# Input transfers, first norm and weight splits at the head of a hybrid decoder step on one Trainium2 core

## The chip, the cores and the metric

The kernel runs on 1 core of one Trainium2 chip. A core has five engines that run their own instruction streams: TensorE (PE in the profile, with its weight loads as PEld), VectorE (DVE), ScalarE (ACT), GpSimd (POOL) and SyncE (SP, which here only issues transfers). 16 DMA engines move data between the chip's memory and the core's SBUF; matmul results lie in PSUM, here eight banks of 128 partitions x 512 float32. The metric is the device time of one execution in microseconds (us), as a median of several runs.

## The reference, cut to what matters

The program is one layer of a decoder trunk with a final norm, for 1024 prompt rows and 64 sample rows (8 sequences of 8) of width 1024. The head of the kernel, with which this change deals, is the first norm and the first gated feed-forward block:

```python
def rmsnorm(x, w):
    xf = x.astype(jnp.float32)
    y = xf * lax.rsqrt(jnp.mean(xf * xf, axis=-1, keepdims=True) + EPS)
    return (y * w.astype(jnp.float32)).astype(x.dtype)

def ffn_half(x, nw, wg, wu, wd):
    h = rmsnorm(x, nw)
    return x + 0.5 * ((jax.nn.silu(h @ wg) * (h @ wu)) @ wd)

def layer(x, q_pos, past, prm, is_prompt):
    x = ffn_half(x, prm['norm_ffn1'], prm['ffn1_wg'], prm['ffn1_wu'], prm['ffn1_wd'])
    h = rmsnorm(x, prm['norm_mix'])
    ...
    x = x + jnp.concatenate([o_att, y_ssm], axis=-1) @ prm['w_out']
    x = ffn_half(x, prm['norm_ffn2'], prm['ffn2_wg'], prm['ffn2_wu'], prm['ffn2_wd'])
```

`wg` and `wu` are 1024 x 2816, `wd` is 2816 x 1024, all float32. Between the two feed-forward blocks stand sparse attention and a state-space mixer, which the change does not touch.

## The kernel before

**Rows.** The 1088 rows (1024 prompt, 64 sample) are kept as columns of transposed tiles. They form two halves of 544 (`HALF`), and each half is cut into a first part of 256 and a second of 288 (`SUBS`, line 27). The four chunks start at rows 0, 544, 256 and 800 and are loaded in that order (`XCHUNKS`, line 29).

**Precision.** A float32 product is made of three passes over rounded numbers. Each operand is split (`split`, line 281) into a high part, a cast on ScalarE (line 267), and a low part, the rest after the cast, by a subtraction on VectorE (line 270). The names are `whi` and `wlo` for weights and `B1h`, `B1l` and so on for the activations. The three passes are the matmuls of lines 412 to 414 in the head, and lines 366 to 368 or 633 to 635 later.

**Products.** Gate, up and down are computed by a scheme with seven products of half-size blocks in place of eight. Each pair of row halves gives seven factors B1 to B7 of which four (1, 2, 4, 3) are blocks of h themselves and the rest are sums and differences. The first pair of weight blocks (`class First`, line 388) works with the four plain blocks alone, so that it can begin while the other factors are still made.

**The head, in order of the code.** `x_load` (line 140) issues the transfers of the x chunks on SP: the first two chunks of 1 MB each, one transfer each (line 146). Then `raw0`, the first 256 columns of `wg` as 1 MB (line 160), then the other two chunks. The first x chunk lies in a buffer that later takes the first weights of `wu` (tag `raw`, two buffers), which are issued when that chunk is done with (line 520).

`begin1` (line 740) makes the norm of the first part of each half: `x_rms` for rows 0 and for rows 544. `x_rms` (line 668) squares each row in two halves of 512 with ScalarE's accumulation (line 677), adds the halves (line 680) and calls `norm_rows` (line 222): scale and add (line 224, VectorE), root (line 225, ScalarE), reciprocal (line 226, VectorE), and matmuls with the identity that spread the inverse over all partitions as `xR` (line 228), from where ScalarE copies it (line 683).

`x_block` (line 685), for kk = 0 to 3, transposes the columns kk and kk + 4 of both halves by matmul (line 693), multiplies by the inverse and the norm's weight to the four blocks h (line 695, VectorE), copies the plain transpose to a stage buffer (`stg`, line 696, ScalarE) and issues its store to `xD` on ScalarE's queue (line 698). `b_quad` (line 292) then splits the four h to B1, B2, B4 and B3. After each block, `g.run` (line 395) splits a quarter of the raw weights and does 24 matmuls; `b_rest` (line 296) makes the other factors. Then `wu` follows for the first part (`u.run`), then the norm and blocks of the second parts, and the remaining weight pairs in `gate_up` (line 463).

**The order on the engines.** Each engine runs its instructions in a fixed order. That order is worked out when the program is built: a planner simulates the program with its own costs and, whenever an engine is free in its simulation, gives it the instruction that stands earliest in the code among those that are ready. So an instruction that is ready early can be placed ahead of one that stands earlier in the code. `tc.issue_after(ins)` adds an edge: instructions made inside it, on the engine of `ins`, are placed behind `ins`. `roots` (line 220) collects the root instructions of the norms for such edges (line 752).

Transposes and squares write to four PSUM banks of tag Y (`banky`), the first gate sums to four of tag X (`bankx`).

Of the kernel before, what the change touches and what calls it, by code (L numbers as in the profile page):

```python
# [3 lines left out]

# [10 lines left out]
AF = mybir.ActivationFunctionType  # L15
OP = mybir.AluOpType
AX = mybir.AxisListType

P = 128
# [6 lines left out]
HALF = T // 2  # L26
# [54 lines left out]
def hybrid_step(ctx: ExitStack, tc: tile.TileContext, *aps):  # L81
    nc = tc.nc
# [57 lines left out]
    def x_load(t0, n):  # L140
        first = not xrows
        xt = (F1R if first else F1).tile([P, 2, DM], F32, name="xt", tag="raw" if first else "Cc",
                                         bufs=2 if first else 3)
        m = min(n, TP - t0, 2 * P) - P
        if m == P:
            nc.sync.dma_start(xt, A["x_prompt"][0, t0:t0 + 2 * P].rearrange("(u p) d -> p u d", p=P))
        else:
            nc.sync.dma_start(xt[:, 0], A["x_prompt"][0, t0:t0 + P])
            nc.sync.dma_start(xt[:m, 1], A["x_prompt"][0, t0 + P:t0 + P + m])
        xrows[t0] = [(xt[:, 0], 0, 0, P), (xt[:, 1], 0, P, m)]  # L150
        if t0 + n == HALF:
            nc.sync.dma_start(xrest[:32], A["x_prompt"][0, t0 + 2 * P:HALF])
            xrows[t0].append((xrest, 0, 2 * P, 32))
        elif t0 + n == T:
            nc.sync.dma_start(xrest[64:], xs2)
            xrows[t0].append((xrest, 64, P + m, 64))
    for t0, n in XCHUNKS[:2]:
        x_load(t0, n)
    raw0 = f32(F1R.tile([P, 8, 2 * P], F32R, name="raw", tag="raw", bufs=2))
    nc.sync.dma_start(raw0, A["ffn1_wg"][0][:, :2 * P].rearrange("(k p) f -> p k f", p=P))  # L160
    for t0, n in XCHUNKS[2:]:
        x_load(t0, n)
    ident = C.tile([P, P], F32, name="ident")
# [23 lines left out]
    def banky(name):  # L187
        return PS.tile([P, 512], F32, name=name, tag="Y", bufs=4)
# [28 lines left out]
    def blocks(n):  # L217
        return [(i, min(P, n - P * i)) for i in range((n + P - 1) // P)]

    roots = []  # L220

    def norm_rows(r, parts, R):

        nc.vector.tensor_scalar(r, r, 1.0 / DM, EPS, op0=OP.mult, op1=OP.add)
        root = nc.scalar.activation(r, r, AF.Sqrt)
        nc.vector.reciprocal(r, r)
        for i, p0, c0, m in parts:
            nc.tensor.matmul(R[:, c0:c0 + m], r[p0:p0 + m, i:i + 1].to_broadcast([m, P]), ident[p0:p0 + m, p0:p0 + m],
                             start=True, stop=True, skip_group_check=True)
        roots.append(root.ins)  # L230
        return R

    def wsplit(W, loads, early=False, dve=False):
# [58 lines left out]
    def b_quad(z, kk, h):  # L292
        for i, src in zip((1, 2, 4, 3), h):
            b_put(z, kk, i, src)
# [373 lines left out]
    def x_rms(t0, n):  # L668
        r = K.tile([P, 3], F32, name=f"xr{t0}", bufs=1)
        r2 = K.tile([P, 2, 3], F32, name=f"xq{t0}", bufs=1)  # L670
        nc.vector.memset(r2, 1.0)
        R = banky("xR")
        parts = []
        for i, (xt, p0, c0, m) in enumerate(xrows[t0]):
            for z in range(2):
                sq = banky("xsq")
                nc.scalar.activation(sq[p0:p0 + m], xt[p0:p0 + m, 512 * z:512 * z + 512], AF.Square,
                                     accum_out=r2[p0:p0 + m, z, i:i + 1])
            parts.append((i, p0, c0, m))
        nc.vector.tensor_tensor(r, r2[:, 0], r2[:, 1], op=OP.add)  # L680
        norm_rows(r, parts, R)
        Rs[t0] = FX.tile("xRs", [P, 288], 2)
        nc.scalar.copy(Rs[t0][:, :n], R[:, :n])

    def x_block(s, kk):
        c0, n = SUBS[s]
        h = []
        for t0 in (c0, HALF + c0):
            stage[t0] = FX.tile("stg", [P, 2, 288], 2)
            for k in (kk, kk + 4):  # L690
                q = banky("x_ps")
                for xt, p0, o, m in xrows[t0]:
                    nc.tensor.transpose(q[:, o:o + m], xt[p0:p0 + m, P * k:P * k + P], ident[p0:p0 + m, p0:p0 + m])
                v = T4[s][:, kk] if len(h) == 1 else FX.tile(f"h{len(h)}", [P, 288], 2)[:, :n]
                nc.vector.scalar_tensor_tensor(v, q[:, :n], w0[:, k:k + 1], Rs[t0][:, :n], op0=OP.mult, op1=OP.mult)
                nc.scalar.copy(stage[t0][:, k // 4, :n], q[:, :n])
                h.append(v)
            stored.append(nc.scalar.dma_start(xD[:, kk::4, t0:t0 + n], stage[t0][:, :, :n]).ins)
        b_quad(s, kk, h)
        h[1] = None  # L700
        return kk, h

    stage, stored = {}, []

    def x_sub(s, product):
        c0, n = SUBS[s]
        T4[s] = F1H.tile([P, 4, n], F32, name=f"T4{s}")
        due = []
        for kk in range(4):
            due.append(x_block(s, kk))  # L710
            product(kk)
            if kk in (1, 2):
                b_rest(s, *due.pop(0))
        return due
# [24 lines left out]

    def begin1():  # L740
        g = First(F1, w1g, silu_out, raw0)
        for t0 in (0, HALF):
            x_rms(t0, SUBS[0][1])
        due = x_sub(0, lambda kk: g.run(0, kk, bankx, True))
        u = First(F1, w1u, times_out(g))
        c0, n = SUBS[1]
        for kk in range(3):
# [1785 lines left out]
```

## Time and profile before

| | us |
|---|---|
| median of 3 runs | 2473.87 |
| lowest and highest of them | 2472.63, 2479.4 |
| the profiled execution | 2475.45 |
| its span, first to last instruction | 2473.8 |

The profile is of one execution. In its rows, a group of like instructions is given with its line, engine, operation, the tile that it writes and those that it reads, and a count; `[x <-ACT y L677]` means that the engine had been idle for x us and that an instruction of line 677 on ScalarE ended the wait. SPq and ACTq are the queues on which SP and ScalarE issue transfers. A stage of the span can be read on its own, with the busy time of every engine and the granted clock of TensorE (1.00 is full speed; the mean of this execution is 0.987). The rows themselves stand in the prediction.

### The profile page before, as it was taken

The page shows a single profiled execution, that of the slowest core. Times are in us where ns is not written, and L with a number is a line of the kernel's source. Part 1 is how long each engine was busy: PE and PEld are TensorE (multiplying, and loading weights), DVE is VectorE, ACT ScalarE, POOL GpSimd, SP SyncE. Part 2 cuts the span into 40 slices and gives each one's busy share as a digit, 9 for nine tenths or more (in the row PEclk, how much of TensorE's full clock was granted, in tenths as well). Part 3 has the DMA queues.
Part 4 walks back from the last instruction along what each step waited for, and adds up shares of the span by engine and source line. Part 5 has one row for each costly group of instructions (what it writes and reads, how often), then busy time and mean ns, then how long its engine had stood idle before and what let it go on. Part 6 is the DMA issues. An engine that isn't in the chain of part 4 may idle for free.

```text
span 2473.8 us, 48193 instructions
## 1 busy us (share of the span) xinstructions
PE 2408.8 (97%) x19026; PEld 2222.8 (90%) x19026; DVE 1744.7 (71%) x3673; ACT 1131.2 (46%) x2501; POOL 418.3 (17%) x533
## 2 busy tenths in 40 slices
PE   7999999999999999999999999999999999999998
PEld 6999999999999998997667766677899999999998
DVE  6777776677778855655656666777967676768776
ACT  7544444441133254425666675444545454543113
POOL 0000000011134343333434343111000000001110
PEclk9999999999999999999999998999999999999999
DMA  4334343598652333423110104476235353559654
GB/s 162 134 133 160 130 164 129 175 338 306 230 190 84 126 116 102 119 69 127 40 64 35 69 35 148 130 250 213 89 123 171 120 174 120 174 213 370 238 209 153
DMA packets 230446, 379.07 MB, mean 153 GB/s; under 512 B 18509, under 2 KB 147705, under 8 KB 228812
## 3 DMA queue, kind: packets, MB, share of 16 engines
q1 hardware_dynamic: 210248, 318.02, 37.7%
q0 software_dynamic: 7600, 38.59, 4.5%
q10 hardware_dynamic: 12372, 19.38, 2.2%
q8 instruction: 150, 2.46, 0.4%
q14 instruction: 76, 0.62, 0.1%
HBM read 255.66 MB, written 124.40 MB: 154 GB/s over the span
## 4 chain that ended last, share of the span: by engine, by line
PE 86%; DVE 6%; DMA 4%; ACT 3%; issue 1%; POOL 0%; ACTq 0%; DVEq 0%; POOLq 0%
PE dq L634 6%; PE gY L367 6%; PE dq L633 6%; PE dq L635 6%; PE gY L368 6%; PE gY L366 6%; PE gX L367 5%; PE gX L366 5%; PE gX L368 5%; PE o L1855 3%; PE pT L1846 3%; PE s L1808 1%; PE xbc L250 1%; PE xbc L251 1%; PE xbc L252 1%; PE cA L1733 1%
## 5 line engine op out<-in xcount | busy, mean ns | idle before, releaser
L634 PE MATMUL dq<-db,da 128*128 128x256 f32 (+1 forms) x1232 | 353.2, 288 | 0.3 <-DVE da L270 0.3
L635 PE MATMUL dq<-db,da 128*128 128x256 f32 (+1 forms) x1232 | 352.8, 288 | 0.0
L633 PE MATMUL dq<-db,da 128*128 128x256 f32 (+1 forms) x1232 | 349.8, 288 | 2.7 <-DVE Cc L386 2.2
L642 DVE TENSOR_TENSOR xT<-xT,dq 128x256 f32<-128x256 f32 (+1 forms) x456 | 186.9, 432 | 84.8 <-PE dq L635 83.2
L270 POOL TENSOR_TENSOR ds<-dw 128x512 f32<-128x512 f32 x22 | 29.5, 1341 | 1228.1 <-DVE wlo L270 508.0
L633 PEld LDWEIGHTS dq<-db,da 128*128 128x128 f32 x1232 | 230.5, 189 | 3.3 <-DVE Cc L386 2.5
L635 PEld LDWEIGHTS dq<-db,da 128*128 128x128 f32 x1232 | 232.8, 189 | 0.0
L634 PEld LDWEIGHTS dq<-db,da 128*128 128x128 f32 x1232 | 231.9, 188 | 0.6 <-DVE da L270 0.5
L267 ACT CAST whi<-ws 128x512 fp32r<-128x512 f32 x156 | 96.5, 623 | 205.9 <-PE gY L368 137.6
L270 DVE TENSOR_TENSOR wlo<-raw,whi 128x512 fp32r<-128x512 f32 x184 | 125.5, 687 | 83.9 <-ACT whi L267 83.5
L267 ACT CAST da<-ds 128x512 fp32r<-128x512 f32 x88 | 52.6, 623 | 234.7 <-PE dq L635 93.4
L267 ACT CAST whi<-raw 128x512 fp32r<-128x512 f32 x181 | 112.4, 626 | 72.0 <-PE g L414 19.5
L270 DVE TENSOR_TENSOR wlo<-ws,whi 128x512 fp32r<-128x512 f32 x156 | 106.7, 687 | 42.4 <-ACT whi L267 41.9
L1824 ACT ACTIVATE pb<-s,mx 128x256 f32<-128x256 f32 (+3 forms) x192 | 105.0, 552 | 59.7 <-DVE mx L1822 37.6
L1846 PEld LDWEIGHTS pT<-ident,pb 128*128 128x128 f32 x528 | 59.6, 143 | 45.8 <-issue 40.1
L1821 DVE TENSOR_REDUCE mx<-s 128x1 f32<-128x384 f32 (+2 forms) x128 | 66.6, 536 | 44.0 <-PE s L1813 34.1
L366 PE MATMUL gY<-B3h,whi 128*128 128x256 f32 (+1 forms) x320 | 91.5, 287 | 1.5 <-ACT whi L267 1.4
L366 PE MATMUL gX<-B6h,whi 128*128 128x256 f32 (+1 forms) x320 | 91.3, 286 | 0.9 <-ACT Cc L373 0.9
L367 PE MATMUL gX<-B6h,wlo 128*128 128x256 f32 (+1 forms) x320 | 91.4, 286 | 0.6 <-DVE wlo L270 0.6
L367 PE MATMUL gY<-B3h,wlo 128*128 128x256 f32 (+1 forms) x320 | 91.6, 287 | 0.2 <-DVE wlo L270 0.2
L277 POOL TENSOR_TENSOR pb<-pb,sm 128x640 f32<-128x640 f32 (+7 forms) x70 | 85.1, 1238 | 37.6 <-DVE sm L1831 34.0
L367 PE MATMUL gY<-B2h,wlo 128*128 128x256 f32 (+1 forms) x320 | 91.4, 286 | 0.0
(763 smaller groups left out, 8548.1 us busy)
## 6 DMA issues: line engine op xcount, KB each, us to landing
db<-GD SPq DMA_DIRECT2D x42, 1632.0 KB
GD<-Cc SPq DMA_DIRECT2D x154, 272.0 KB
GD<-his SPq DMA_DIRECT2D x84, 272.0 KB
raw<-in_ffn_wu_dram SPq DMA_DIRECT2D x22, 1024.0 KB
dw<-in_ffn_wd_dram SPq DMA_DIRECT2D x44, 512.0 KB
raw<-in_ffn_wg_dram SPq DMA_DIRECT2D x21, 1024.0 KB
GD<-hp SPq DMA_DIRECT2D x70, 272.0 KB
db<-GD SPq DMA_DIRECT2D x14, 1088.0 KB
```

The costliest lines, as they stand in the source:

```text
L267: return nc.scalar.copy(out, src) if eng == "a" else ENGINES[eng].tensor_copy(out, src)
L270: ENGINES[eng].tensor_tensor(out, x, y, op=op)
L277: nc.gpsimd.tensor_tensor(out, x, by.to_broadcast(list(x.shape)), op=OP.mult)
L366: nc.tensor.matmul(q, ah[:, k], b_, start=first, stop=False, skip_group_check=True)
L367: nc.tensor.matmul(q, al[:, k], b_, start=False, stop=False, skip_group_check=True)
L368: nc.tensor.matmul(q, ah[:, k], c_, start=False, stop=(k == 3), skip_group_check=True)
L633: nc.tensor.matmul(q, x, bh[:, u, o], start=first, stop=False, skip_group_check=True)
L634: nc.tensor.matmul(q, y, bh[:, u, o], start=False, stop=False, skip_group_check=True)
L635: nc.tensor.matmul(q, x, bl[:, u, o], start=False, stop=(u == np_ - 1), skip_group_check=True)
L642: nc.vector.tensor_tensor(x, x, q, op=OP.subtract if i == 4 else OP.add)
L1824: nc.scalar.activation(pb[:, st:st + pn], s, AF.Exp, bias=mx[:, 0:1], accum_out=part[:, hh_, i:i + 1])
L1846: nc.tensor.transpose(tq_[:kn, P * hh_:P * hh_ + P], src, ident)
```

## The change

Five edits, all in the head.

1. The chunks of x that start a half (rows 0 and 544) come in two transfers of 128 rows each. The first weights come in four transfers: transfer k brings the row blocks k and k + 4, which `g.run` for kk = k reads.
2. In `x_rms`, the second half of each row is squared on VectorE (`tensor_tensor_reduce`) where the chunk starts a half; ScalarE squares the first half.
3. The norm of a chunk is made inside `x_block`, when its rows are first needed: the block of rows 0 stands ahead of the norm of rows 544.
4. The splits of h (`b_quad`) and the split of the first weights stand behind the second norm's root on ScalarE and behind its reciprocal on VectorE.
5. The weight splits for kk = 1 to 3 stand behind the last stage copy (ScalarE) and the last h (VectorE) of the block before.

```diff
@@ x_load
-        if m == P:
+        if t0 % HALF and m == P:
             nc.sync.dma_start(xt, A["x_prompt"][0, t0:t0 + 2 * P].rearrange("(u p) d -> p u d", p=P))
         else:
             nc.sync.dma_start(xt[:, 0], A["x_prompt"][0, t0:t0 + P])
@@
-    nc.sync.dma_start(raw0, A["ffn1_wg"][0][:, :2 * P].rearrange("(k p) f -> p k f", p=P))
+    for k in range(4):
+        nc.sync.dma_start(raw0[:, k::4], A["ffn1_wg"][0][:, :2 * P].rearrange("(k p) f -> p k f", p=P)[:, k::4])
@@
-    roots = []
+    roots, inverses = [], []
+
+    @contextmanager
+    def behind(pair):
+        with tc.issue_after(pair[0]), tc.issue_after(pair[1]):
+            yield
@@ norm_rows
-        nc.vector.reciprocal(r, r)
+        inverse = nc.vector.reciprocal(r, r)
...
         roots.append(root.ins)
+        inverses.append(inverse.ins)
@@ x_rms
-                sq = banky("xsq")
-                nc.scalar.activation(sq[p0:p0 + m], xt[p0:p0 + m, 512 * z:512 * z + 512], AF.Square,
-                                     accum_out=r2[p0:p0 + m, z, i:i + 1])
+                sq, x = banky("xsq")[p0:p0 + m], xt[p0:p0 + m, 512 * z:512 * z + 512]
+                if z and t0 % HALF == 0:
+                    nc.vector.tensor_tensor_reduce(out=sq, in0=x, in1=x, scale=1.0, scalar=0.0, op0=OP.mult,
+                                                   op1=OP.add, accum_out=r2[p0:p0 + m, z, i:i + 1])
+                else:
+                    nc.scalar.activation(sq, x, AF.Square, accum_out=r2[p0:p0 + m, z, i:i + 1])
@@ x_block
         for t0 in (c0, HALF + c0):
+            if t0 not in Rs:
+                x_rms(t0, n)
...
-                nc.vector.scalar_tensor_tensor(v, q[:, :n], w0[:, k:k + 1], Rs[t0][:, :n], op0=OP.mult, op1=OP.mult)
-                nc.scalar.copy(stage[t0][:, k // 4, :n], q[:, :n])
+                made = nc.vector.scalar_tensor_tensor(v, q[:, :n], w0[:, k:k + 1], Rs[t0][:, :n],
+                                                      op0=OP.mult, op1=OP.mult)
+                staged = nc.scalar.copy(stage[t0][:, k // 4, :n], q[:, :n])
                 h.append(v)
+            ends[s, kk] = staged.ins, made.ins
...
-        b_quad(s, kk, h)
+        with behind((roots[1], inverses[1])):
+            b_quad(s, kk, h)
...
-    stage, stored = {}, []
+    stage, stored, ends = {}, [], {}
@@ begin1
-        for t0 in (0, HALF):
-            x_rms(t0, SUBS[0][1])
-        due = x_sub(0, lambda kk: g.run(0, kk, bankx, True))
+        def gate(kk):
+            with behind(ends[0, kk - 1] if kk else (roots[1], inverses[1])):
+                g.run(0, kk, bankx, True)
+        due = x_sub(0, gate)
```

More of the change, by code (lines that the diff above doesn't have):

```diff
@@ L1 @@
 import itertools
-from contextlib import nullcontext
+from contextlib import contextmanager, nullcontext
 from contextlib import ExitStack
```

## The prediction

> **What bounds the kernel now.** First the page: busy time by engine, and the chain of work that ended last by engine.
>
> ```profile
> PE 2408.8 (97%) x19026; PEld 2222.8 (90%) x19026; DVE 1744.7 (71%) x3673; ACT 1131.2 (46%) x2501; POOL 418.3 (17%) x533
> ...
> PE 86%; DVE 6%; DMA 4%; ACT 3%; issue 1%; POOL 0%; ACTq 0%; DVEq 0%; POOLq 0%
> ```
>
> TensorE is busy for 2408.8 of 2473.8 us, so 65.0 us in all can be won by filling its gaps. Next, the busy time by stage (columns: stage, length, then busy us and instructions of PE, PEld, DVE, ACT, POOL, granted clock, DMA share, GB/s).
>
> ```profile
> 0.00:16.00 16.00, 2.45 (x9) 2.10 (x10) 4.30 (x19) 9.13 (x25) 0.96 (x8) 1.00 0.90 320
> 16.00:36.00 20.00, 16.88 (x123) 15.02 (x122) 19.24 (x53) 14.82 (x46) 0.00 (x0) 1.00 0.54 169
> 36.00:62.00 26.00, 24.73 (x181) 21.31 (x179) 19.34 (x53) 22.07 (x62) 0.00 (x0) 1.00 0.19 58
> 62.00:73.00 11.00, 9.77 (x39) 8.55 (x40) 11.00 (x30) 5.92 (x17) 0.00 (x0) 0.53 0.24 83
> 73.00:90.00 17.00, 17.00 (x130) 17.00 (x130) 9.53 (x19) 8.58 (x19) 0.00 (x0) 1.00 0.46 142
> 90.00:2474.00 2384.00, 2337.98 (x18553) 2158.81 (x18551) 1681.34 (x3502) 1070.69 (x2336) 417.37 (x525) 0.99 0.45 153
> ```
>
> The change touches the head alone. There TensorE does 2.45 us of work in the first 16 us: the norm's inverse is late. From 16 to 36 VectorE is full (19.24 of 20) and TensorE waits for its low parts; from 36 on TensorE is nearly full. So the head is worth what it can start earlier, and every later stage follows as it is, if nothing in it is tied to absolute time. The timeline says why the head starts late (start, length, engine, line, output<-inputs, count, idle time before and what ended it).
>
> ```profile
> 0.83 0.95 SPq L146 DMA_DIRECT2D xt<-in_x_prompt_dram  x2
> ...
> 1.82 0.47 SPq L160 DMA_DIRECT2D raw<-in_ffn_wg_dram  x1
> ...
> 5.92 0.60 ACT L677 ACTIVATE xsq<-xt 128x512 f32<-128x512 f32 x1 [2.93 <-DMA xt<-in_x_prompt_dram]
> ...
> 8.51 0.16 DVE L680 TENSOR_TENSOR xr<-xq 128x3 f32<-128x3 f32 x1 [5.68 <-ACT xsq L677]
> ...
> 9.02 0.58 ACT L677 ACTIVATE xsq<-xt 128x512 f32<-128x512 f32 x1
> 9.15 0.18 DVE L226 RECIPROCAL xr<-xr 128x3 f32<-128x3 f32 x1 [0.27 <-ACT xr L225]
> ...
> 11.47 0.35 ACT L683 COPY xRs<-xR 128x256 f32<-128x256 f32 x1
> ...
> 11.72 2.18 ACT L267 CAST whi<-raw 128x512 fp32r<-128x512 f32 x4
> 11.79 0.17 DVE L224 TENSOR_SCALAR xr<-xr 128x3 f32<-128x3 f32 x1
> 12.37 2.50 DVE L270 TENSOR_TENSOR wlo<-raw,whi 128x512 fp32r<-128x512 f32 x4 [0.41 <-ACT whi L267]
> 13.80 0.20 ACT L225 ACTIVATE xr<-xr 128x3 f32<-128x3 f32 x1
> 14.79 0.17 DVE L226 RECIPROCAL xr<-xr 128x3 f32<-128x3 f32 x1
> 15.01 1.22 PE L228 MATMUL xR<-ident,xr 128*128 128x128 f32 x4 [4.41 <-DVE xr L226]
> ...
> 16.70 0.48 DVE L695 SCALAR_TENSOR_TENSOR h<-x_ps,w,xRs 128x256 f32<-128x256 f32 x1 [1.74 <-PE x_ps L693]
> ...
> 17.62 0.88 DVE L695 SCALAR_TENSOR_TENSOR h<-x_ps,w,xRs 128x256 f32<-128x256 f32 x2
> ...
> 18.41 0.42 DVE L270 TENSOR_TENSOR B1l<-h,B1h 128x256 fp32r<-128x256 f32 x1
> ```
>
> ScalarE waits for the first whole megabyte of x until 5.92, then squares eight half rows alone, four for each norm. The second norm's sum is scaled at 11.79, yet its root comes only at 13.80: four weight casts (11.72 to 13.80) stand ahead of it on ScalarE. Its reciprocal comes at 14.79, as four low parts (12.37 to 14.87) stand ahead of it on VectorE. The first h follows at 16.70.
>
> **The change part by part.**
>
> *Smaller transfers.* When would the pieces land? The DMA view of the first 18 us, in 40 slices of 0.45 us:
>
> ```profile
> GB/s 0 0 0 0 118 27 255 400 428 428 419 392 391 400 419 419 437 355 378 380 355 344 355 391 364 437 410 391 400 401 319 264 364 382 401 218 246 300 246 9
> DMA packets 2255, 5.51 MB, mean 306 GB/s; under 512 B 135, under 2 KB 1167, under 8 KB 2255
> ```
>
> Adding slices, 1.05 MB have moved at 5.25; the square starts at 5.92, so about 0.6 us pass between last byte and use (estimate). If the transfers run in the order of their issue, 0.52 MB are through at 4.0, 1.57 at 6.55, 2.10 at 7.8; the four half transfers are then usable at 4.6, 5.9, 7.15 and 8.4, the four weight quarters at 9.1, 9.8, 10.6 and 11.3 (2.36, 2.62, 2.88 and 3.15 MB at 8.5, 9.2, 10.0 and 10.7). SP issues eight instead of three at 0.47 us each, done by about 4.6, ahead of the data; bytes are the same. The other chunks stand behind them on SP as before; the last slices show them in by 18, and their first square comes at 31.73 (row further down). I cost the issues at nothing. If the pieces land only together, the norms' blocks are there at 5.9 and 8.4, and the second norm ends about 0.6 us later, since its two squares on each engine then follow each other.
>
> [...]
>
> From these rows the fixed part of the first transfer is 1.9 us ahead of its data (issued at 0.83, data from the slice at 2.7 on) and 0.6 behind it. Yet from 3.15 to 13.5 the slices run on at 344 to 437 GB/s across the borders of the transfers, so I take it as overlapped.
>
> *Half the squares on VectorE.* A square on ScalarE goes by 0.61 us (5.92 to 8.51 for four). The tensor_tensor_reduce is not in the trace; its nearest rows are a two-input instruction of the same width, and a custom one, and a wider one with three inputs:
>
> ```profile
> L270 DVE TENSOR_TENSOR wlo<-raw,whi 128x512 fp32r<-128x512 f32 x5 | 3.2, 686 | 0.4 <-ACT whi L267 0.4
> ...
> L2080 DVE CUSTOM_DVE_ANT_0 S<-s_ps,big 128x512 f32<-128x512 f32 x20 | 13.7, 685 | 3.1 <-PE s_ps L2077 3.0
> ...
> L1056 DVE SCALAR_TENSOR_TENSOR acc<-xr,vec,acc 128x1024 f32<-128x1024 f32 x24 | 35.5, 1480 | 0.2
> ```
>
> I take 0.69, with ends of 0.69 and 1.48; VectorE is idle there (4.30 of 16 us busy), so the four cost nothing unless they are slow. First norm: second block at 5.9, squares done at 6.6, then what runs from 8.51 to 9.33 before (add, scale, root, reciprocal: 0.82, with 0.03 to start): 7.45. Second: block at 8.4, squares 9.1, inverse 9.95; call it 10.0, with a little for the first norm's copy. Before: 14.96. At 1.48 each, four from 4.6 on that wait for their data end at 10.1, and the inverse at 11.0.
>
> *Casts and low parts behind the second inverse, block 0 of x ahead of the second norm.* The four casts leave the path to the root (2.1 us), the four low parts that to the reciprocal (0.99 us from the root's start to the reciprocal's). After the inverse the order xR, copy, h stays: 1.74 us (14.96 to 16.70), so the second pair of h starts at 11.75. The first pair (2 x 0.43 us, as four took from 16.70 to 18.41) is now done before it, and B1l, B2l (2 x 0.36, the mean of 53 in 19.24 us) and the first low part (0.62, a quarter of 2.50) fit into the 1.74. Of VectorE's stretch that ran from 16.70 to 36.0, 1.6 us are thus done ahead; but three low parts (3 x 0.62 = 1.9 us) that lay in idle time before now lie inside it. It ends at 11.75 + 19.3 - 1.6 + 1.9 = 31.35, 4.65 us earlier. If nothing is done ahead, 32.95: 3.05 us. If everything hides, 10.0 against 14.96: 4.96 us. I take 4.5, a little under the sum, as the stretch is 96% and not wholly full. Moved casts: three of 0.52 us on ScalarE, which has 5.2 us free from 16 to 36.
>
> What is late next? The up projection's first weights:
>
> ```profile
> 18.19 0.63 ACTq L698 DMA_DIRECT2D xD<-stg  x1
> ...
> 20.81 0.65 ACT L696 COPY stg<-x_ps 128x256 f32<-128x256 f32 x2 [0.46 <-DMA xD<-stg]
> ...
> 27.18 0.38 SPq L520 DMA_DIRECT2D raw<-in_ffn_wu_dram  x1
> ...
> 31.16 0.38 ACT L696 COPY stg<-x_ps 128x256 f32<-128x256 f32 x1 [1.78 <-DMA xD<-stg]
> ...
> 31.73 0.61 ACT L677 ACTIVATE xsq<-xt 128x512 f32<-128x512 f32 x1
> ...
> 33.81 0.43 DVE L267 CAST whi<-raw 128x512 fp32r<-128x512 f32 x1
> ```
>
> They take the buffer of the first x chunk, so they are issued when its last transposes are done (27.18) and are used at 33.81. Both are tied to the blocks, not to the clock, and move with them. The waits added order only ScalarE and VectorE: behind the held casts stand the casts of B and the stage copies, which need the inverse themselves.
>
> *Sum.* 2475.45 (the profiled execution, span 2473.8 and 1.65 around it) - 4.5 = 2470.95. The shown median, 2473.87, lies 1.58 below that execution; so the predicted median is **2469.4**, a change of 0.18%. Less than 0.3%, 7.4 us, can't be told from no change here.
>
> **The rivals.**
>
> *The clock drop goes.* Shorter windows (columns as above):
>
> ```profile
> 28.00:30.00 2.00, 1.11 (x10) 0.94 (x8) 2.00 (x7) 1.05 (x3) 0.00 (x0) 1.00 0.98 271
> ...
> 61.00:62.00 1.00, 0.22 (x2) 0.11 (x1) 1.00 (x4) 0.64 (x2) 0.00 (x0) 1.00 0.00 0
> 62.00:63.00 1.00, 0.00 (x0) 0.00 (x0) 1.00 (x3) 0.27 (x2) 0.00 (x0) 0.72 0.00 0
> 63.00:64.00 1.00, 0.77 (x3) 0.44 (x3) 1.00 (x4) 0.57 (x3) 0.00 (x0) 0.50 0.00 0
> ...
> 72.00:73.00 1.00, 1.00 (x7) 1.00 (x7) 1.00 (x4) 0.00 (x0) 0.00 (x0) 0.66 0.00 0
> ```
>
> After a gap of 2 us TensorE runs at 0.50 for 10 us, and falls behind by up to 4.7 us of work. VectorE is full until 73, so not all of it counts: 130 matmuls stood after 73, 96 of them the up product that comes last anyway; at full clock some 23 of the other 34 would have been done, 23 x 0.131 = 3.0 us (between 0 and 4.5). If the shifted gap causes no drop: 2466.4. For it: the gap is only 2 us long, and the equally poor stretch from 28 to 30 kept 1.00. Against: nothing in the change fills the gap itself, which ends with a VectorE that is full.
>
> [...]
>
> *Stores collide.* xD's stores start near 10 instead of 18.2, while the x chunks still fill the engines until 17. A stage copy that waits as at 31.16 (1.78 us) once early in VectorE's stretch: gain 2.7, 2471.2. For it: DMA share 0.90 up to 16. Against: VectorE has queued low parts to do meanwhile.
>
> *The smaller transfers pay their fixed part one after the other.* That part of the change would not do what it says. Two more transfers stand ahead of the second norm's data, at 1.9 + 0.6 us from the rows above: 5.0 us, more than the 4.5 won: 2474.4. Against it: the slices.
>
> *A second clock drop*, the slower side. Place: the stretch where TensorE starves today (16 to 36, 16.88 of 20), which starts on a colder engine and ends 4.5 us earlier. A drop like the one at 62.7 reaching into the full stretch behind it (36 to 62, 24.73 of 26) costs half its length there: 10 us cost 5.0 us, 2474.4. It decides from 9 us of half clock in that stretch on.
>
> **How the numbers follow.** Forecast 0.52; drop gone 0.20; collision 0.14; transfers 0.06; second drop 0.08. Faster by over 0.3% (below 2466.45): two thirds of the drop's 0.20, and 0.05 of the forecast's (its gain at 4.96 with part of the drop gone): 0.18. Slower by over 0.3%: two drops, 0.03. Within: 0.79. Range: from the drop gone at its full 4.5 us (2464.9) with a little below, 2464.5, to the second drop with 1 us for the scatter of the runs, 2475.4.
>
> **What would show it.** Second reciprocal (L226) at 10 instead of 14.79; L677 split between ACT and DVE at 0.69; low parts of raw spread over VectorE's stretch; the weights of L520 issued near 22.7; every row of the later stages 4.5 us earlier. Wrong if the squares on VectorE cost over 2.3 us (four in a row would put the inverse back to 14.7), if the shift is lost between 31 and 90, or if TensorE's clock differs there.

## The result and the profile after

The changed kernel takes **2485.72 us** (median of 9 runs, 2482.65 to 2494.15) beside 2472.63 us (9 runs, 2467.98 to 2479.4) of the kernel before: a ratio of 1.0055, 95% interval 1.0043 to 1.0068. So it is slower by some 13 us, where 2469.4 was forecast; the whole range ended at 2475.4. The profiled execution took 2482.97 us, with a span of 2481.3. In the series of the experiments below five executions, of the kernel before too, took far longer (2641.69 to 8135.65 us); the medians count them, the ratios do not.

A note on lines: the diff shifts them. Lines 224 to 228 are now 230 to 234, the casts and low parts (267, 270) 274 and 277, the squares 688 (ScalarE) and 685 (VectorE), the stage copy 709, the store 712, the first weights of `wu` 527, and everything behind the head stands 16 lines further down.

First the head. The timeline of the kernel after, for the norms and what follows them:

```profile
4.49 0.70 DVE L685 CUSTOM_DVE_ANT_0 xsq<-xt 128x512 f32<-128x512 f32 x1 [2.48 <-DMA xt<-in_x_prompt_dram]
...
5.76 0.70 DVE L685 CUSTOM_DVE_ANT_0 xsq<-xt 128x512 f32<-128x512 f32 x1 [0.49 <-DMA xt<-in_x_prompt_dram]
...
7.83 0.60 ACT L688 ACTIVATE xsq<-xt 128x512 f32<-128x512 f32 x1 [0.59 <-DMA xt<-in_x_prompt_dram]
...
8.58 0.70 DVE L685 CUSTOM_DVE_ANT_0 xsq<-xt 128x512 f32<-128x512 f32 x1 [1.14 <-ACT xsq L688]
...
9.37 0.60 ACT L688 ACTIVATE xsq<-xt 128x512 f32<-128x512 f32 x1 [0.24 <-DVE xq L685]
...
11.19 0.63 ACTq L712 DMA_DIRECT2D xD<-stg  x1
...
11.29 0.18 DVE L232 RECIPROCAL xr<-xr 128x3 f32<-128x3 f32 x1 [0.27 <-ACT xr L231]
...
19.94 0.65 ACT L709 COPY stg<-x_ps 128x256 f32<-128x256 f32 x2 [1.89 <-DMA xD<-stg]
...
24.78 0.38 SPq L527 DMA_DIRECT2D raw<-in_ffn_wu_dram  x1
```

The squares start as soon as the smaller pieces land, and VectorE's take 0.70 us. But the third and fourth wait for one another (1.14 and 0.24 us, put down to a square or its sum, no longer to a transfer), and the second reciprocal ends at 11.47: 3.5 us earlier than before (14.96), not 5. At 19.94 a stage copy waits 1.89 us for a store. The stages, with the columns of before:

```profile
0.00:16.00 16.00, 6.79 (x33) 6.33 (x34) 9.52 (x36) 9.47 (x26) 0.95 (x8) 1.00 0.90 317
16.00:36.00 20.00, 14.60 (x100) 12.74 (x99) 17.92 (x47) 15.32 (x47) 0.00 (x0) 0.90 0.57 173
36.00:62.00 26.00, 25.41 (x178) 22.36 (x176) 17.42 (x49) 18.43 (x51) 0.00 (x0) 0.94 0.17 56
62.00:73.00 11.00, 8.83 (x50) 7.76 (x50) 11.00 (x30) 6.88 (x19) 0.00 (x0) 0.84 0.24 83
73.00:90.00 17.00, 17.00 (x131) 17.00 (x129) 10.93 (x23) 8.83 (x20) 0.00 (x0) 1.00 0.46 142
```

TensorE has been busy for 6.79 us by 16, where it had been for 2.45. Then the granted clock, which before was 1.00 up to 62, shows 0.90 and 0.94: there is a new drop in the first part, and the one from 62 to 73 is smaller (0.84 for 0.53). So the head wins something and gives part of it back. None of it is a loss of 13 us.

**Where the time goes.** To find it, each TensorE instruction of one trace is looked up in the other (by line, tiles and how often it has occurred), and the starts are subtracted. The median over each stretch:

| stretch, us | after, against before |
|---|---|
| 16 to 20 | 4.3 us earlier |
| about 28 | 3.4 earlier |
| 44 to 68 | 1.0 later |
| 90 to 450 | 1.23 earlier, the same for every instruction |
| 1050 to 1130 | 0.76 later |
| 1400 to 1530 | 7 to 8.5 later, and scattered |
| 1750 to 2150 | 5.4 later |
| the end | 7.4 later |

The head ends 1.23 us ahead, and that stands unchanged for 360 us. Most of the time is lost between about 1130 and 1500 us: the attention of the prompt rows, a stage that no edit touches. (Smaller steps stand near 1000 and 2200 us. From 1500 to 1600 the kernel before loses some itself: its clock is 0.90 there, against 0.95 after.) There the shift is not one number: some instructions come 9 us earlier and others 18 us later, so they run in **another order**. Counted from the two programs' instruction lists, 2790 of the 17116 TensorE instructions behind the head stand in another place, all of them in the mixer and nearly all in its two attention stages; in the feed-forward blocks none does. The planner, which fills each engine from its own simulation, had come to that stage with another history.

### The profile page after: what moved, and what is told of

Same layout as the page of the kernel before. It is cut to its first block, busy times and chain, and to the rows that moved or that the text cites. A ratio compares the mean times of both kernels' runs of the same rounds, so it can differ in the third digit from the quotient of the medians.

```text
span 2481.3 us, 48202 instructions
## 1 busy us (share of the span) xinstructions
PE 2413.9 (97%) x19026; PEld 2227.6 (90%) x19026; DVE 1750.7 (71%) x3681; ACT 1129.3 (46%) x2493; POOL 416.1 (17%) x533
## 4 chain that ended last, share of the span: by engine, by line
PE 85%; DVE 5%; DMA 5%; ACT 3%; issue 1%; POOL 0%; ACTq 0%; SPq 0%; DVEq 0%; POOLq 0%
PE gY L374 6%; PE gY L375 6%; PE gY L373 6%; PE dq L641 6%; PE dq L640 6%; PE dq L642 6%; PE gX L374 5%; PE gX L373 5%; PE gX L375 5%; PE o L1871 3%; PE pT L1862 3%; PE xbc L257 1%; PE s L1824 1%; PE xbc L258 1%; PE xbc L259 1%
## 5 line engine op out<-in xcount | busy, mean ns | idle before, releaser
L375 PE MATMUL gX<-B6l,whi 128*128 128x256 f32 (+1 forms) x320 | 92.0, 287 | 0.0
L373 PE MATMUL gY<-B2h,whi 128*128 128x256 f32 (+1 forms) x320 | 91.4, 286 | 0.0
```

Of the source, the lines that this page charges most:

```text
L373: nc.tensor.matmul(q, ah[:, k], b_, start=first, stop=False, skip_group_check=True)
L375: nc.tensor.matmul(q, ah[:, k], c_, start=False, stop=(k == 3), skip_group_check=True)
```

## The experiments

Two theories. **The order theory**: the 13 us come from the new order of instructions far behind the edits; the edits themselves win a little. **The head theory**, its rival: they come from the edits, by what they do on the chip. Beside these, smaller questions on what the head gave back.

To part the two, an experiment holds the order of everything behind the head. A helper adds a planning edge between each instruction and the next on its engine, for a list of instructions; the edges order but do not wait:

```diff
+def pin_order(nc, tc):
...
+    traced = list(nc.cur_bb.bb.instructions)
+    for steps in json.loads(zlib.decompress(base64.b85decode(_ORDER))).values():
+        at = list(itertools.accumulate(steps))
+        for a, b in zip(at, at[1:]):
+            tc.add_manual_dep(traced[b], traced[a].name, mybir.DependencyInfo(
+                mybir.DependencyClass.NoSync, mybir.DependencyReason.DATA), reason="pin_order")
```

`_ORDER` holds the wanted order, engine by engine. "Held in before's order" means that everything behind the head runs in the order that the kernel before has there; the head is planned freely. The expectations call the constant distance to the kernel before, from 130 us on, the plateau. Each ratio below is against runs of the kernel before in the same series (medians 2471.88, 2472.46 and 2472.32 us in the three series; 2472.63 beside the changed kernel).

| experiment | head | order behind it | median us | ratio, 95% interval |
|---|---|---|---|---|
| the changed kernel | after | after | 2485.72 | 1.0055 [1.0043, 1.0068] |
| e1 | after | before | 2473.65 | 1.0005 [0.9996, 1.0014] |
| e2 | before | after | 2484.02 | 1.0044 [1.0029, 1.0059] |
| e5 | before | after in the prompt rows' attention alone | 2487.39 | 1.0072 [1.0052, 1.0092] |
| e6 | before | after in the sample rows' attention and what follows it | 2476.05 | 1.0016 [1.0006, 1.0025] |
| e3 | after, VectorE squares in other banks | before | 2468.91 | 0.9992 [0.9981, 1.0003] |
| e4 | after, late x chunks behind the stores | before | 2475.23 | 1.0012 [0.9998, 1.0026] |
| e10 | as e3, `wu` in four transfers | before | 2470.68 | 0.9990 [0.9974, 1.0006] |
| e9 | the smaller transfers alone | before | 2467.97 | 0.9993 [0.9980, 1.0005] |
| v1 | the smaller transfers alone | planned freely | 2469.25 | 0.9994 [0.9975, 1.0014] |
| v2 | the squares alone | planned freely | 2473.47 | 1.0009 [0.9994, 1.0023] |
| e7 | the order edits alone | before | 2472.98, one run | none |
| e8 | the squares alone | before | 2471.63, one run | none |

### e1: the changed head with the old order behind it

The edit is the helper above, in the changed kernel, with before's order.

> The changed kernel, with every instruction after the head held in the order that each engine had in the kernel before. Theory A (the planner, whose simulated times moved with the head, gave the middle of the kernel another order, and that order costs about 14 us): the time falls from 2485.7 to about 2471, the head's 1.2 us under the kernel before. Theory B (the changed head itself makes TensorE's clock drop more often, and the order is no matter): about 2485, as the changed kernel. In the trace of A each instruction from 130 us on stands at one constant distance from the kernel before, up to the end, but for single clock drops.

Measured: 1.0005 [0.9996, 1.0014]. The 13 us are gone, and the edits are all still there. In its trace each instruction stands 1.5 us ahead of before's from 90 to 450 us, and 2.2 to 2.5 us ahead from 1050 to 1400; the scatter of the changed kernel is not there. The head theory falls.

### e2: the old head with the new order behind it

The same helper in the kernel before, with the order of the changed kernel.

> The other half: the kernel before with its old head, and everything after the head in the order that the changed kernel has. Theory A: the loss comes without any edit of the head, 2472.6 + 14 = about 2486. Theory B: about 2472, as before.

Measured: 1.0044 [1.0029, 1.0059], from a kernel that has none of the five edits. The two experiments together show the cause from both sides: the order behind the head costs 11 to 12 us, and the edits cost nothing that can be measured.

### e5 and e6: which part of the order

The mixer has two attention stages whose order differs. In e5 only that of the prompt rows (about 1100 to 1560 us) has the new order, in e6 only that of the sample rows (about 1650 to 1750) and of what follows it. Both have the head of before.

> The kernel before, its head unchanged; only the instructions of the prompt's attention (in the code from its preparation up to the sample group's attention) stand in the order that the changed kernel gave them, everything else in the old order. If the loss of 12 us that e2 showed sits in this stretch: about 2484, and the distance to the kernel before grows between 1000 and 1560 us. If it sits in the sample group's attention: about 2472.

> As e5 with the other part: only the instructions of the sample group's attention and after it stand in the changed kernel's order. About 2472 if the prompt's stretch holds the loss, about 2484 if this one does; both between if they share it. e5 and e6 together should give e2's 12 us.

Measured: e5 1.0072 [1.0052, 1.0092], e6 1.0016 [1.0006, 1.0025]. The order of the prompt rows' attention alone costs all that the full change costs (the intervals overlap); that of the sample rows' costs some 4 us by itself. The two do not add up to e2's 11 us, as e6's expectation had it: 18 and 4 are more than that, and why is open.

What is poor about that order can be read in one stretch, 1300 to 1400 us. Busy time and clock there, of before:

```profile
1300.00:1400.00 100.00, 98.17 (x698) 74.51 (x697) 63.26 (x148) 64.85 (x176) 37.98 (x55) 1.00 0.12 43
```

of the changed kernel:

```profile
1300.00:1400.00 100.00, 94.81 (x640) 70.66 (x639) 61.27 (x140) 59.85 (x161) 34.40 (x52) 0.97 0.12 43
```

of e1 (changed head, old order):

```profile
1300.00:1400.00 100.00, 98.60 (x690) 73.49 (x688) 63.29 (x149) 64.54 (x176) 36.01 (x54) 1.00 0.12 43
```

and of e5 (old head, new order):

```profile
1300.00:1400.00 100.00, 94.81 (x642) 70.06 (x642) 61.36 (x141) 61.37 (x163) 37.62 (x53) 0.98 0.12 43
```

The first number after the length is TensorE's busy time: 98.2 and 98.6 with the old order, 94.81 and 94.81 with the new one, whichever head stands ahead. The granted clock is 1.00 with the old and 0.97 or 0.98 with the new; but e7 and e8 below, which have the old order and TensorE busy for 98.60 us there, show 0.98 too, so the busy time is the sign that goes with the order. What TensorE waits for in that stretch (tile and line waited on; total us, times, longest), before:

```profile
PE s L1808 <- ACT pb L1824: 0.7, 1, 0.7
PE cA L1733 <- ACT th L267: 0.7, 1, 0.7
PE pT L1846 <- ACT pt L267: 0.4, 1, 0.4
```

after:

```profile
PE s L1824 <- ACT pb L1840: 1.7, 3, 0.8
PE cT L1728 <- DVE vcs L1764: 1.1, 2, 0.9
PE cT L1728 <- DVE sm L1846: 1.0, 1, 1.0
PE c L1759 <- DVE cxh L1430: 0.6, 1, 0.6
PE cT L1728 <- DVE mx L1838: 0.2, 1, 0.2
PE pT L1862 <- ACT pt L274: 0.2, 1, 0.2
```

and e5:

```profile
PE s L1808 <- ACT pb L1824: 1.7, 3, 0.8
PE cT L1712 <- DVE vcs L1748: 1.1, 2, 0.9
PE cT L1712 <- DVE sm L1830: 1.0, 1, 1.0
PE c L1743 <- DVE cxh L1414: 0.6, 1, 0.6
PE cT L1712 <- DVE mx L1822: 0.2, 1, 0.2
PE pT L1846 <- ACT pt L267: 0.2, 1, 0.2
```

The waits of after and e5 are the same to a tenth, 16 lines apart. TensorE waits 4.8 us instead of 1.8 there. The timeline says what lies behind the waits at `cT`. In this stage a sample sequence's cache is compressed between the attention products: GpSimd gathers a piece `chk`, copies bring it into `chp`, TensorE transposes it (`cT`) and multiplies it (`cA`). Before, the gather and the first copy that uses it:

```profile
1321.70 1.01 POOL L1689 DMA_INDIRECT chk<-in_cache_cmp_dram,idx  x1 [0.27 <-POOL chp L267]
1331.38 0.39 POOL L267 COPY chp<-chk 128x256 f32<-128x256 f32 x1 [8.67 <-DMA chk<-in_cache_cmp_dram,idx]
```

and after:

```profile
1327.47 1.01 POOL L1705 DMA_INDIRECT chk<-in_cache_cmp_dram,idx  x1 [1.15 <-ACT chp L274]
1336.27 0.39 POOL L274 COPY chp<-chk 128x256 f32<-128x256 f32 x1 [4.71 <-DMA chk<-in_cache_cmp_dram,idx]
...
1379.24 1.01 POOL L1705 DMA_INDIRECT chk<-in_cache_cmp_dram,idx  x1 [0.15 <-issue]
```

From issue to use it takes some 9 us in both (9.7 and 8.8). The gather is issued 6 us later in the new order, the next one at 1379.24 instead of 1365.39: the compression, whose products fill TensorE between the softmax steps, falls behind, and TensorE's gaps end with a softmax row (`pb`) or with VectorE work ahead of `cT`. The gaps are of 1 us or less, and the clock drops among them: 0.68 from 1340 to 1350 in the changed kernel. That this gather is the one instruction to blame was not tried; it is read from the trace, and so is the clock's part.

How much is clock and how much is waiting? Each run lists its span and mean granted clock; span x (1 - clock) is the time in which TensorE was held back, counted at full clock. Means over the runs:

| kernel | span | span x (1 - clock) | the rest |
|---|---|---|---|
| before (28 runs) | 2471.1 | 29.1 | 2441.9 |
| e1, after with the old order (12) | 2471.3 | 30.1 | 2441.3 |
| after (9) | 2484.6 | 39.2 | 2445.4 |
| e2, before with the new order (6) | 2481.9 | 34.3 | 2447.6 |
| e5, new order in the prompt rows' attention (6) | 2487.2 | 35.7 | 2451.6 |

With the new order both grow: 5 to 10 us of lost clock and 3.5 to 10 us of the rest. The split goes by the recorded clock alone and cannot say which of the two brings the other. In the profiled executions of after and e1, which have the same head, the shift between the two grows from 3.3 to 13.3 us from 1050 to 1600; the other 5.7 us of their 15.9 come in three steps, near 1000, 1700 and 2200 us.

### v1 and v2: does any new order cost time?

One edit alone, with nothing held: in v1 the smaller transfers, in v2 the squares on VectorE. Either build too gets another order, with over 1000 TensorE instructions in another place.

> The same edit of the transfers alone, but with nothing held: the planner orders everything behind the head anew. Theory (any small edit of the head makes the planner find another order in the mixer, and that order sets the time, whatever the edit was for): the time differs by more than 3 us from that of the same edit with the order held, in either direction. Rival (only the order of the full change is a bad one, small edits leave the time alone): within 2 us of it, so 2470 to 2474 us.

> The squares of each row's second half on VectorE alone, with nothing held: the planner orders everything behind the head anew. Theory (as for the transfers): more than 3 us away from the kernel before, in either direction, although its head differs by a us at most. Rival: within 2 us of the kernel before.

Measured: 0.9994 [0.9975, 1.0014] and 1.0009 [0.9994, 1.0023]; v1 is 1.3 us from e9, the same edit held in before's order. My expectation missed and the rival's times hold. But the traces show less than the question asks. From 1000 to 1559 us both builds run TensorE's instructions in the very order of the kernel before; the places that differ lie at 755 to 765 us and from 1560 us on, nearly all in the sample rows' attention. So the stage whose order costs the time in e5 was not reordered here, and TensorE is busy for over 98 us in 1300 to 1400, as before. The two show that edits of the head can reorder a stage far behind them at no cost that can be told; whether another new order of the prompt rows' attention would also be dear, no run shows.

### e3: the squares in other banks

The VectorE squares write to banks of tag X, which stand idle so early, and no longer share the four banks of tag Y with ScalarE's squares and the transposes. Order held as in e1.

```diff
-                sq, x = banky("xsq")[p0:p0 + m], xt[p0:p0 + m, 512 * z:512 * z + 512]
+                sq, x = (bankx if z and t0 % HALF == 0 else banky)("xsq")[p0:p0 + m], xt[p0:p0 + m, 512 * z:512 * z + 512]
```

> As e1, and VectorE's squares of the first two chunks go to the other four PSUM banks. In the changed kernel the second norm's squares took turns: VectorE's waited 1.14 us for one of ScalarE's to end, and the second inverse came at 11.47 instead of the 10.0 predicted. Theory A1 (the four shared banks make them take turns): the second inverse ends near 10.0 to 10.3, and the plateau from 130 us on moves by up to 1.2 us. Rival (the data land later than estimated): inverse stays at 11.5. Time 2470, within the scatter of e1.

The timeline of e3, VectorE's four squares and the second reciprocal:

```profile
4.54 0.70 DVE L685 CUSTOM_DVE_ANT_0 xsq<-xt 128x512 f32<-128x512 f32 x1 [2.53 <-DMA xt<-in_x_prompt_dram]
...
5.81 0.70 DVE L685 CUSTOM_DVE_ANT_0 xsq<-xt 128x512 f32<-128x512 f32 x1 [0.50 <-DMA xt<-in_x_prompt_dram]
...
7.28 0.70 DVE L685 CUSTOM_DVE_ANT_0 xsq<-xt 128x512 f32<-128x512 f32 x1 [0.23 <-DMA xt<-in_x_prompt_dram]
...
8.60 0.70 DVE L685 CUSTOM_DVE_ANT_0 xsq<-xt 128x512 f32<-128x512 f32 x1 [0.53 <-DMA xt<-in_x_prompt_dram]
...
10.68 0.17 DVE L232 RECIPROCAL xr<-xr 128x3 f32<-128x3 f32 x1
```

Now each square waits for its data alone, and the inverse is there at 10.85 instead of 11.47. So 0.6 us of the 1.5 us by which it missed 10.0 were the shared banks (e1, which differs from e3 in the banks alone, ends its second inverse at 11.48). The rest is what the planner placed ahead in the norm's chain: the root ends at 10.06, the reciprocal starts at 10.68 behind two h of the first pair on VectorE. The head leads by 3.45 us at 100 us, and no clock drop shows between 16 and 62. 2468.91 us is 3 us under before's median, with an interval that includes 1: the best version of the full change, but not one that is shown to beat the kernel before.

### e4: the collision of loads and stores

The last two x chunks are issued behind the fourth store, and the first four stores go out on SP's queue. Order held.

```diff
-    def x_load(t0, n):
+    def x_load(t0, n, later=None):
...
+            queue = nc.sync if s == 0 and kk < 2 else nc.scalar
+            stored.append(queue.dma_start(xD[:, kk::4, t0:t0 + n], stage[t0][:, :, :n]).ins)
+        if s == 0 and kk == 1:
+            with tc.issue_after(stored[-1]):
+                for a in pending:
+                    nc.sync.dma_start(*a)
```

> As e1, with the last two chunks of x issued behind the fourth store of the first part, so that they do not share the DMA engines with the stores (the first four stores go to the queue of SP for that). Theory A2 (the stores collide with these loads: stage copy waits 1.89 us at 19.94, TensorE starves and its clock drops in 20 to 40): the wait and the drop go, the plateau from 130 us on lies at -3.5 to -5 us from the kernel before instead of -1.2, and the time is 2 to 3 us under e1. Rival (VectorE bounds that stretch whatever the stores do): plateau near -1.2 as in e1.

The wait at 20 us is gone, so it was the loads or the queue that held the stores; the edit changes both. But the gain missed: the instructions at 90 to 450 us stand 2.67 us behind before, not 3.5 to 5 ahead. The loads now go out from 19.8 to 23 us, beside the later stores and the first weights of `wu`. The timeline and a window of e4:

```profile
33.22 0.65 ACT L712 COPY stg<-x_ps 128x256 f32<-128x256 f32 x2 [4.59 <-DMA xD<-stg]
```

```profile
26.00:36.00 10.00, 3.05 (x20) 2.85 (x19) 5.88 (x17) 2.88 (x9) 0.00 (x0) 0.72 0.88 256
```

TensorE has 3.05 us of work in these 10. The collision is moved, not avoided: 1.0012 [0.9998, 1.0026].

### e10: the first weights of `wu` in four transfers

As e3, with line 527's first transfer cut in four, so that the first cast need not wait for the whole megabyte.

```diff
-            load = nc.sync.dma_start(raw, src)
+                for k in range(4):
+                    load = nc.sync.dma_start(raw[:, k::4], src[:, k::4])
```

> As e3, and the first weights of the up projection also come in four transfers of a quarter, as those of the gate do. Theory (the up product waits for the whole megabyte, TensorE has 0.66 of 2 us busy from 30 to 32 in e3): its first cast starts 1 to 2 us earlier and the plateau from 130 us on goes from -3.45 to about -5; time about 2467. Rival (VectorE's stretch is what ends last there): plateau stays at -3.4, time as e3, 2469.

Missed in the profiled execution, which stands 0.73 us behind before at 100 us. Its windows say why:

```profile
36.00:62.00 26.00, 24.48 (x146) 20.34 (x145) 16.76 (x45) 18.97 (x53) 0.00 (x0) 0.77 0.17 52
62.00:73.00 11.00, 11.00 (x50) 8.98 (x51) 10.46 (x28) 4.75 (x13) 0.00 (x0) 0.60 0.16 55
```

The clock is lost for 0.23 x 26 + 0.40 x 11 = 10.4 us there, where before loses 5.2 in its one drop. Over all runs the ratio is 0.9990 [0.9974, 1.0006]: nothing that can be told from e3.

### e7, e8, e9: each edit alone

Each has one part of the change, the old order behind the head, and nothing else: e7 the order edits (3 to 5), e8 the squares, e9 the transfers.

> The order edits alone (norm inside the block, splits behind the second inverse), old transfers and squares on ScalarE, everything after the head in the old order. By the prediction's terms the root no longer waits for four casts nor the reciprocal for four low parts: second reciprocal at about 12.0 to 12.5 instead of 14.79, plateau from 130 us on near -2. Rival (the stores' collision and the clock drop eat it): plateau near 0 or above.

> Only the squares of each row's second half go to VectorE; transfers, casts and low parts as in the kernel before, and everything behind the head held in the order of the kernel before. Theory (each edit has its own share of the head's gain, and the order edits hold most of it; the squares alone cannot, as x still lands in whole megabytes): second reciprocal ends between 13.5 and 15.0 us (14.96 before, 11.47 with all edits), instructions at 90 to 450 us between 1.0 us earlier and 0.5 us later than before. Rival (the squares are what brings the head's gain): reciprocal ends by 12.5.

> Only the smaller transfers of x and of the first weights; everything else as in the kernel before, and everything behind the head held in the order of the kernel before. Theory (the order behind the head is the cost, the head is worth a few us at most): 2472 us, between 2469 and 2475, ratio 0.998 to 1.001; second reciprocal ends between 13.5 and 15.0 us. Rival (the smaller transfers cost time of their own, somewhere): over 2476 us.

The second reciprocal in the timelines of e7,

```profile
12.77 0.18 DVE L231 RECIPROCAL xr<-xr 128x3 f32<-128x3 f32 x1 [0.27 <-ACT xr L230]
```

of e8,

```profile
10.84 0.18 DVE L231 RECIPROCAL xr<-xr 128x3 f32<-128x3 f32 x1 [0.27 <-ACT xr L230]
```

and of e9:

```profile
12.82 0.17 DVE L232 RECIPROCAL xr<-xr 128x3 f32<-128x3 f32 x1
```

| edits | second inverse ends | lead at 100 us |
|---|---|---|
| none (before) | 14.96 | 0 |
| order edits alone (e7) | 12.95 | 1.92 |
| transfers alone (e9) | 12.99 | 2.15 |
| squares alone (e8) | 11.02 | 2.52 behind |
| all (after) | 11.47 | 1.23 |
| all, other banks (e3) | 10.85 | 3.45 |

For e8 the expectation fell and its rival holds: the squares alone bring the inverse 3.9 us earlier. The pieces of x still land as whole megabytes there, but with both engines squaring, the last root stands at 10.61, ahead of the first weight cast at 11.58. The casts that held the root before are then behind it without any edge. So the gains do not add up: each edit removes the same wait in another way, and all five together end the inverse later (11.47) than the squares alone. And the lead at 100 us does not follow the inverse alone. The clock counts too: e8's 16 to 73 us lose 12.8 us of it, before's 5.2 (each window's length times what its clock lacks to 1.00).

## Why the prediction was wrong

**The step that failed** is "every later stage follows as it is, if nothing in it is tied to absolute time". With the old order held they do follow (e1: 1.5 us ahead at 90 to 450 us, 2.2 to 2.5 from 1050 to 1400); in the changed kernel they did not. Their order is made by the planner, in code order from whatever is ready in its simulation, and an edit in the head is an edit of that simulation's history. The kernel's description says so, and the prediction used it for the head, but priced it at nothing for the stages behind. e1, e2 and e5 show that this one term is 11 to 18 us by their ratios and holds the whole result. None of the rivals named it; the forecast and its four rivals all looked at the first 90 us.

**The head's own terms.**
- *Landing of the pieces*: estimated 4.6, 5.9, 7.15 and 8.4; e3's squares start at 4.54, 5.81, 7.28 and 8.60. Right there; in the changed kernel's own trace the third piece is usable only at 7.83.
- *Transfers that pay their fixed part in series* (the rival at 0.06): wrong. The pieces of 0.52 MB are usable 1.27, 1.47 and 1.32 us apart in e3, that is at 357 to 413 GB/s, and the rate of the whole megabytes before was 344 to 437. The prediction read 1.9 us ahead of the data and 0.6 behind it off the first transfer; the pieces, issued one behind the other on SP's queue, follow each other by little more than half of those 2.5 us, so that part was not paid in full for each of them there.
- *Square on VectorE*: 0.69 taken, 0.70 measured. Right. An instruction of 0.14 that reads the sum follows it, its start 0.08 ahead of the square's end. (The sum for the upper price of 1.48 is wrong: four in a row from 4.6 on end at 10.5 and not at 10.1, and the inverse would come at 11.4. The forecast does not use it.)
- *Second inverse at 10.0*: 11.47. Mis-sized by 1.5 us: 0.6 for the shared banks (e3), which the prediction did not look at, the rest for work that the planner placed in the norm's chain, and data 0.2 us later.
- *The lead of 4.5 us*: 1.23 in the profiled execution at 90 to 450 us, 1.5 in e1. Beside the late inverse, two of the rivals came true in the place that they named. **Stores collide**: 1.89 us at 19.94, against 1.78 taken. **A second clock drop** in the stretch from 16 to 62: the windows of the changed kernel show it.

```profile
28.00:30.00 2.00, 0.59 (x6) 0.39 (x4) 2.00 (x6) 1.89 (x7) 0.00 (x0) 1.00 1.03 345
30.00:32.00 2.00, 1.13 (x7) 0.93 (x8) 1.12 (x5) 1.75 (x5) 0.00 (x0) 1.00 0.36 118
32.00:34.00 2.00, 0.64 (x4) 0.41 (x4) 1.36 (x4) 2.00 (x8) 0.00 (x0) 0.55 0.59 169
34.00:36.00 2.00, 2.00 (x10) 2.00 (x11) 1.66 (x4) 2.00 (x7) 0.00 (x0) 0.50 0.11 1
36.00:38.00 2.00, 2.00 (x12) 2.00 (x11) 2.00 (x8) 0.46 (x2) 0.00 (x0) 0.50 0.45 132
38.00:40.00 2.00, 2.00 (x15) 2.00 (x15) 1.07 (x5) 0.41 (x2) 0.00 (x0) 0.75 0.09 1
```

TensorE is busy for 2.36 us of the six from 28 to 34, and the clock is halved from 32.2 us on (0.55 in 32 to 34) for 6.8 us, some 3.4 us of work. TensorE's gaps there end with casts on ScalarE; how much of them goes back to the stores, x and `wu` on the DMA engines (share 1.03 at 28 to 30) was not tried apart. Besides, the products that the change brings ahead of 15 us started 0.21 us apart, against 0.12 from 15.68 on (last section), which neither the prediction nor the clock column has. The prediction has the stretch from 16 on start "on a colder engine"; that this brings a drop was its estimate, and no run shows it. Against that, the drop at 62 to 73 shrank (0.53 to 0.84), the first rival's half. In all, the head's clock loss from 16 to 73 is 5.3 us after and 5.2 before.
- *Later rows 4.5 us earlier, L520 near 22.7*: the weights of `wu` were issued at 24.78 (27.18 before).

With the order held (e1), the time is 2473.65, inside the range and 4 us over the forecast. Beside the kernel before of its own series (2471.88) the head's gain of 4.5 us is not there: the interval allows at most 1 us.

## What to carry to other kernels

Where a planner orders the program, an edit is never local: compare the instruction order of the untouched stages before the times, and hold that order when an edit is to be judged, or a run of the edit measures the planner's luck with it. Several edits that remove the same wait do not add: try each alone, and stop at the one that removes it (here half the squares on another engine brought the inverse earlier than all five edits). And a lead won at the start counts at the end only if the engine that bounds the kernel is kept fed on the way there (here 1.23 us ahead at 90 to 450 us became 7.4 behind at the end).

## What the runs showed of the hardware

- One and the same head got another clock in other executions. before, e2, e5 and e6 share their head; at 100 us they stand 0, 0.12 later, 1.99 later and 0.92 earlier. e5's window from 36 to 62 shows how, beside 1.00 in the same window before:

```profile
36.00:62.00 26.00, 25.53 (x167) 22.08 (x166) 16.91 (x45) 20.37 (x57) 0.00 (x0) 0.87 0.19 59
```

  Over 28 runs of the kernel before, the time lost to the clock is 29.1 us with a standard deviation of 4.3, while the rest varies by 2.9. A gain of 2 us in the head is inside that.
- The clock drops had lengths in steps of 3.41 us. In the clock records of the traces of before and after, every drop is to 0.50. Those of before last 3.41 us (three), 6.83 (two), 10.24 (two) and 13.65 (one), those of after 3.41 (seven), 6.83 (three) and 10.24 (two); the last drop of each, of 10.34 and 7.16 us, ends with the record. Within each of the two traces the starts lie multiples of 3.41 us apart. What sets the start of a drop, no run shows.
- At a granted 1.00 the first products took longer than later ones. The same product of 128x256 in the changed kernel at a granted 1.00, 1.00 and 0.50:

```profile
14.25 0.41 PE L420 MATMUL g<-B1h,wlo 128*128 128x256 f32 x1
...
15.68 0.28 PE L420 MATMUL g<-B4h,wlo 128*128 128x256 f32 x1
...
34.10 0.42 PE L420 MATMUL g<-B4h,wlo 128*128 128x256 f32 x1
```

  The first one took about as long as the one at 0.50 (0.41 and 0.42 us): the next matmul starts 0.21 us behind it, against 0.12 behind the one at 15.68 and 0.22 behind the one at 34.10. In the changed kernel this spacing changes between 14.89 and 15.68 us, in before between 18.02 (0.22 to the next) and 18.24 (0.12). So an early start of the products was worth less here than the clock column says; what sets the moment of the change, no run shows.
- In the changed kernel TensorE's clock fell behind gaps of under 2 us. Its gaps from 28 us on are 1.75 us (up to 30.34) and 0.53 (up to 31.61), and the clock falls to 0.50 at 32.2; a gap of 1.36 us begins only after that, at 32.37. At 1339.5 it fell behind gaps of 0.82, 0.60 and 0.40 us, just as a fourth began (0.94 us; window 1340 to 1350: 0.68). How much idle time it takes, and whether idle time is the cause, no run here shows.
